# Branch outputs loaded into the buffer of their lower parts and split there; queries of a head loaded once

## The chip, the core and the metric

The program runs on one core of a Trainium2 chip. The core has a matrix engine (PE, with a separate queue for loading weights, PEld), a vector engine (DVE), a scalar engine (ACT), GpSimd (POOL), and SyncE (SP), from which nearly all transfers of this program are issued to 16 shared DMA engines. The metric is the device time of one execution in microseconds, the median over several runs.

## What is computed

One layer of an encoder over two sequences, of 1024 and 2048 tokens, each with 16 learned tokens in front. Only the skeleton is shown; all arithmetic is float32.

```python
xn = _rmsnorm(h, g_pre)
proj = xn @ w_in + b_in                      # 1024 -> 6672 columns
na_q, na_k, na_v, na_z, ml_qk, ml_v, ml_z, ml_o, ml_g, mg = jnp.split(proj, SPLIT_IDX, axis=-1)
ya = _neighbourhood_attention(q, k, v, na_rpb)   # 8 heads of 64, windows of 8 x 16 on a grid 64 wide
ya = (ya * silu(na_z)) @ w_a
yb = (_mlstm_branch(ml_qk, ml_v, ml_g, ml_o, conv_w, head_g) * silu(ml_z)) @ w_b   # 4 heads of 128
ga, gb = split(sigmoid(mg))
y = (ga * ya + gb * yb) @ w_out
return h + _rmsnorm(y, g_post)
```

## The kernel before

To keep float32 accuracy each operand of a matmul is split in two: an upper part, which ACT makes by copying to a shorter format (`yh`, `xh`, `whi`, `mh`), and a lower part, the rest, which DVE makes by subtracting (`yl`, `xl`, `wlo`, `mlo`). A product is three matmuls, upper by upper, upper by lower, lower by upper (L155 to L157, L577 to L579, L1497 to L1499).

Two generators run beside each other. `dense` makes the projections and the end of the layer; `sparse` makes the mLSTM branch (`ml`) and the attention (`na`). `run` takes steps of both in turn, by costs written in the code, and this fixes the order of the PE's instructions. The order on the other engines and on SP's queue is made by a planner when the program is built: it plays the program through with its own times, and an instruction whose data and buffers are ready by these times may be put far ahead of its place in the code. Each queue then runs in that order, and an instruction that has to wait holds up all that stand behind it on its engine.

The end of the layer is `final(s, b, nxt)`, six blocks of 512 tokens: two of the first sequence, four of the second. A block has two stages. In the first, called the branch stage here, the outputs of both branches (`y`, eight slices k of 128 features; k = 4 to 7 are the mLSTM's, k = 0 to 3 the attention's) are multiplied by `w_a` and `w_b`, gated (DVE, L1467 and L1469) and split into `mh` and `mlo` (ACT L1470, DVE L1471). In the second, the output projection, `mh` and `mlo` are multiplied by `w_out` in 16 units of 128 tokens by 256 columns, each followed by ACT L1524 and DVE L1525. While the blocks are made the attention of the second sequence still runs, 32 heads one after another; one query block of a head takes the PE through scores (L849), ACT through the exponential (L857), DVE through scaling (L866), the PE through a transpose (L874), ACT and DVE through the split of the result (L876, L877), and the PE and both again through the output (L886, L890, L892).

`yload(s, b)` brings the outputs of the branches from DRAM for a block. It is started in the output projection of the block before (for the first block in the last projection job before it), and stepped once for each unit (`hook`). Before, a slice is loaded to a buffer `yr` (L1418) with the tag `st`, which has four buffers that the gates `tg` and other stages use as well; when three slices are under way the oldest is split: ACT copies `yr` to `yh[:, k]` (L1405), DVE subtracts into `yl[:, k]` (L1406). The buffers `yh` and `yl` share their tags with `xh` and `xl`, two each: the next block's `yl` takes the place of this block's `yl`, which is free when the branch stage has ended.

`na_prep` prepares a head of the attention one head ahead. `twice` loads a matrix of 64 rows to both halves of the partitions, which is used for the queries (`qr`, L733 twice) and the keys (`kr`). ACT then copies `qr` to `stk` on 128 partitions (L824), copies the upper 64 partitions' result to `qB` (L826), and DVE subtracts on partitions 64 to 127, so that `stk` holds upper parts above and lower parts below (L827). Keys go the same way (L829, L831), values in L834 and L836.

Of the kernel before, what the change touches and what calls it, by code (L numbers as in the profile page):

```python
# [9 lines left out]
F32 = mybir.dt.float32  # L10
F32R = mybir.dt.float32r
I32 = mybir.dt.int32
AF = mybir.ActivationFunctionType
ALU = mybir.AluOpType
# [3 lines left out]
P = 128  # L18
# [102 lines left out]
class K:  # L121
# [671 lines left out]
    def na_prep(self, np_, s, rows, heads, j):  # L793

        nc, i = self.nc, self.i
        rt, pr, hh = heads[j]
        typ, lo, nr = rows[rt]
        ns, h0 = nr + 1, hh * 64
        ms, rs = ((nr, 0), (nr, 0), (0, 1))[typ]
        qr = np_.tile([P, 512], F32, name="qr", bufs=1)  # L800
        stk = np_.tile([P, 4, P], F32R, name="stk", bufs=2)
        qb = self.qB[hh]
        self.twice(qr, self.NQ[s][pr], h0, rt * 512)
        sv = stk.rearrange("p b t -> p (b t)")
        kr = np_.tile([P, 16, 64], F32, name="kr", bufs=1)
        kd = np_.tile([P, 16, 64], F32R, name="kd", bufs=2)
        kx = self.kx[hh]
        self.twice(kr[:, rs:rs + nr, :].rearrange("p a b -> p (a b)"), self.NK[s][pr], h0, lo * 64)
        self.twice(kr[:, ms, :], self.NKM[pr], h0, 0)
        ks = 8 * ns  # L810
        if hh == 0:
            self.vr = np_.tile([P, 8, P], F32, name="vr", bufs=1)
            f0 = pr * P
            nc.sync.dma_start(self.vr[ms * 8:ms * 8 + 8], self.NVM[:, f0:f0 + P].rearrange("(b c) f -> c b f", c=8))
            nc.sync.dma_start(self.vr[rs * 8:(rs + nr) * 8],
                              self.NV[s][:, lo * 8:(lo + nr) * 8, f0:f0 + P].rearrange("b q f -> q b f"))
            self.zt = np_.tile([P, 512], F32, name="zt", bufs=2)
            nc.sync.dma_start(self.zt, self.NZ[s][pr][:, rt * 512:(rt + 1) * 512])
            self.yg = np_.tile([P, 512], F32, name="yg", bufs=2)
        vr, zt, yg = self.vr, self.zt, self.yg  # L820
        if j < 2 or rows[heads[j - 2][0]][0] != typ:
            nc.gpsimd.dma_start(kx[64:128, :ns, :].rearrange("p a b -> p (a b)"), i["masks"][typ, :, :ns * 64])
        yield
        nc.scalar.activation(sv, qr, AF.Copy)  # L824
        yield
        nc.scalar.activation(qb[0:64], stk[0:64].bitcast(F32), AF.Copy)  # L826
        nc.vector.tensor_tensor(sv[64:128], qr[64:128], sv[64:128].bitcast(F32), op=ALU.subtract)  # L827
        yield
        nc.scalar.activation(kd[:, :ns, :], kr[:, :ns, :], AF.Copy)  # L829
        yield  # L830
        nc.vector.tensor_tensor(kx[0:64, :ns, :], kr[0:64, :ns, :], kd[0:64, :ns, :].bitcast(F32), op=ALU.subtract)  # L831
        vt = np_.tile([P, 8, 2, 64], F32R, name="vt", bufs=2)
        vv = vr[:ks, :, h0:h0 + 64]
        nc.scalar.activation(vt[:ks, :, 0], vv, AF.Copy)  # L834
        yield
        nc.vector.tensor_tensor(vt[:ks, :, 1], vv, vt[:ks, :, 0].bitcast(F32), op=ALU.subtract)  # L836
        self.head = stk, qb, kd, vt, yg, zt
        yield
# [556 lines left out]
    def yload(self, s, b):  # L1395

        nc, fp, n = self.nc, self.wp, 512
        yh = fp.tile([P, KT, n], F32R, name="yh", tag="xh", bufs=2)
        yl = fp.tile([P, KT, n], F32R, name="yl", tag="xl", bufs=2)
        self.y, self.yk = ((s, b), yh, yl), set()  # L1400
        todo = deque()

        def split():
            k, yr = todo.popleft()
            nc.scalar.activation(yh[:, k], yr, AF.Copy)  # L1405
            nc.vector.tensor_tensor(yl[:, k], yr, yh[:, k].bitcast(F32), op=ALU.subtract)  # L1406
            self.yk.add(k)

        for k in (4, 5, 6, 7, 0, 1, 2, 3):
            need = ("ml", s) if k > 3 else ("na", s, b, k)  # L1410
            if need not in self.done:
                while todo:
                    split()
                    yield
                while need not in self.done:
                    yield "wait"
            yr = fp.tile([P, n], F32, name="yr", tag="st", bufs=4)
            nc.sync.dma_start(yr, self.YA[s][b][k][:, :] if k < 4 else self.YB[s][k - 4][:, b * n:(b + 1) * n])  # L1418
            todo.append((k, yr))
            if len(todo) == 3:  # L1420
                split()
                yield
        while todo:
            split()
            yield

    def ystart(self, s, b):
        self.ygen = self.yload(s, b)
# [269 lines left out]
```

## Time and profile before

| | |
|---|---|
| median of 3 runs | 2843.53 us (2842.91 to 2847.38) |
| the profiled execution, its own time | 2845.39 us |
| its span, first to last instruction | 2843.6 us |
| granted clock of the PE, mean | 0.994 |
| DMA | 661.42 MB, mean 233 GB/s |

The profile's page gives the busy time of each engine. The view of stretches gives the same for any window, with the clock that the PE was granted (1.00 is full) and the mean busy share of the DMA engines. The view of waits sums the idle time of an engine by the line that waited and the work that ended the wait: total us, number of times, longest. In the view in order of time a row has its start, its duration, engine and line, and in square brackets the idle time of that engine just before it and what ended this.

### The profile page before, as it was taken

What the parts mean: (1) busy time and instruction counts of PE and PEld (TensorE: products, weight loads), DVE (VectorE), ACT (ScalarE), POOL (GpSimd) and SP (SyncE); (2) the same over time, 40 slices, a digit from 0 to 9 for tenths busy, and PEclk for the clock granted to TensorE, in tenths of its full rate; (3) what the DMA queues carried; (4) which work ended last, traced back from release to release, by engine and by line L of the source; (5) the groups of instructions that cost most, each with busy time, mean ns of one, the idle gap of its engine ahead of it and who ended that gap; (6) DMA issues with size and microseconds to landing.
All of it is one profiled execution on the core that took longest, in us unless ns stands there. A gap on an engine that the chain in (4) does not pass through costs nothing.

```text
span 2843.6 us, 49257 instructions
## 1 busy us (share of the span) xinstructions
PE 2795.7 (98%) x17312; PEld 2488.8 (88%) x17312; DVE 1796.3 (63%) x4931; ACT 1306.4 (46%) x3135; POOL 16.1 (1%) x103
## 2 busy tenths in 40 slices
PE   9999999999999999999999999999999999999998
PEld 8998898999899988888988888888888988889898
DVE  5233678576456654456667566474679888787854
ACT  5122546444444443355455555453455554545421
POOL 0000000000000000000000000000000000000000
PEclk9999999999999999999999999999999999999999
DMA  9554768765966554685656776656679999897875
GB/s 373 186 186 178 261 210 300 252 196 165 343 210 192 169 173 131 189 281 181 210 176 224 251 274 193 185 171 180 196 239 355 308 308 279 286 291 258 290 259 193
DMA packets 382120, 661.42 MB, mean 233 GB/s; under 512 B 51664, under 2 KB 200608, under 8 KB 381872
## 3 DMA queue, kind: packets, MB, share of 16 engines
q1 hardware_dynamic: 380752, 655.58, 69.7%
q0 software_dynamic: 1120, 2.69, 0.4%
q8 instruction: 137, 2.24, 0.3%
q14 instruction: 111, 0.91, 0.1%
HBM read 455.90 MB, written 202.22 MB: 231 GB/s over the span
## 4 chain that ended last, share of the span: by engine, by line
PE 85%; DMA 8%; DVE 5%; ACT 1%; issue 1%; SPq 0%; DVEq 0%; ACTq 0%
PE pj L155 15%; PE pj L156 14%; PE pj L157 14%; PE pj L577 6%; PE pj L578 6%; PE pj L579 6%; PE pj L1499 3%; PE pj L1497 3%; PE pj L1498 3%; PE sm L886 3%; PE tr L874 2%; DMA wlo<-wl 1%; DMA um<-ud 1%; PE sm L157 1%; PE sc L849 1%; PE sm L156 1%
## 5 line engine op out<-in xcount | busy, mean ns | idle before, releaser
L155 PE MATMUL pj<-xh,whi 128*128 128x512 f32 (+1 forms) x1792 | 705.7, 394 | 0.9 <-ACT whi L250 0.9
L156 PE MATMUL pj<-xl,whi 128*128 128x512 f32 (+1 forms) x1792 | 689.5, 385 | 0.1
L157 PE MATMUL pj<-xh,wlo 128*128 128x512 f32 (+1 forms) x1792 | 688.2, 384 | 0.3 <-DVE wlo L251 0.3
L577 PE MATMUL pj<-whi,xh 128*128 128x256 f32 (+3 forms) x1576 | 451.2, 286 | 4.4 <-DMA whi<-wh 2.9
L578 PE MATMUL pj<-wlo,xh 128*128 128x256 f32 (+3 forms) x1576 | 445.1, 282 | 0.8 <-DMA wlo<-wl 0.8
L579 PE MATMUL pj<-whi,xl 128*128 128x256 f32 (+3 forms) x1576 | 444.6, 282 | 0.0
L157 PEld LDWEIGHTS pj<-xh,wlo 128*128 128x128 f32 x1792 | 337.2, 188 | 72.1 <-DVE wlo L251 0.5
L155 PEld LDWEIGHTS pj<-xh,whi 128*128 128x128 f32 x1792 | 337.7, 188 | 60.5 <-ACT whi L250 1.7
L156 PEld LDWEIGHTS pj<-xl,whi 128*128 128x128 f32 x1792 | 338.0, 189 | 56.9 <-issue 1.0
L577 PEld LDWEIGHTS pj<-whi,xh 128*128 128x128 f32 (+1 forms) x1576 | 294.5, 187 | 6.4 <-DMA whi<-wh 3.1
L578 PEld LDWEIGHTS pj<-wlo,xh 128*128 128x128 f32 (+1 forms) x1576 | 294.3, 187 | 2.1 <-DMA wlo<-wl 1.1
L579 PEld LDWEIGHTS pj<-whi,xl 128*128 128x128 f32 (+1 forms) x1576 | 294.3, 187 | 0.9
L1497 PE MATMUL pj<-whi,mh 128*128 128x256 f32 x768 | 220.9, 288 | 4.2 <-DMA whi<-wh 2.4
L1499 PE MATMUL pj<-whi,mlo 128*128 128x256 f32 x768 | 217.5, 283 | 1.1 <-DVE mlo L1471 1.1
L1498 PE MATMUL pj<-wlo,mh 128*128 128x256 f32 x768 | 217.5, 283 | 0.1
L857 ACT ACTIVATE prb<-sc,mx 128x384 f32<-128x384 f32 (+2 forms) x192 | 119.8, 624 | 204.2 <-DVE mx L853 193.2
L877 DVE TENSOR_TENSOR pts<-tr,pts 96x512 fp32r<-96x512 f32 (+2 forms) x192 | 131.5, 685 | 75.8 <-ACT pts L876 74.3
L876 ACT ACTIVATE pts<-tr 96x512 fp32r<-96x512 f32 (+2 forms) x192 | 113.9, 593 | 114.8 <-PE tr L874 113.5
L155 PE MATMUL pj<-yh,whi 128*128 128x512 f32 x384 | 155.9, 406 | 0.0
L156 PE MATMUL pj<-yl,whi 128*128 128x512 f32 x384 | 152.2, 396 | 0.0
L157 PE MATMUL pj<-yh,wlo 128*128 128x512 f32 x384 | 152.2, 396 | 0.0
L1497 PEld LDWEIGHTS pj<-whi,mh 128*128 128x128 f32 x768 | 146.3, 190 | 6.5 <-ACT mh L1470 2.3
(271 smaller groups left out, 5049.4 us busy)
## 6 DMA issues: line engine op xcount, KB each, us to landing
whi<-wh SPq DMA_DIRECT2D x176, 512.0 KB
wlo<-wl SPq DMA_DIRECT2D x176, 512.0 KB
wraw<-wu SPq DMA_DIRECT2D x64, 512.0 KB
wh<-whi SPq DMA_DIRECT2D x64, 512.0 KB
wl<-wlo SPq DMA_DIRECT2D x64, 512.0 KB
gt<-st SPq DMA_DIRECT2D x96, 256.0 KB
tg<-gt SPq DMA_DIRECT2D x96, 256.0 KB
xt<-xt SPq DMA_DIRECT2D x32, 512.0 KB
```

The lines of the kernel that those rows point to most:

```text
L155: mm(out, ah, bh, start=start, stop=False)
L156: mm(out, ah, bl, start=False, stop=False)
L157: mm(out, al, bh, start=False, stop=stop)
L577: nc.tensor.matmul(o, xh, wh, start=k == 0, stop=False)
L578: nc.tensor.matmul(o, xh, wl, start=False, stop=False)
L579: nc.tensor.matmul(o, xl, wh, start=False, stop=k == KT - 1)
L857: nc.scalar.activation(pr_[:, :N].rearrange("p (b a c) -> p b a c", b=4, c=8), sc[:, :N].rearrange("p (a b c) -> p b a c", b=4, c=8), AF.E ...
L876: nc.scalar.activation(pts[:ks, :, 0, :], pt[:ks], AF.Copy)
L877: nc.vector.tensor_tensor(pts[:ks, :, 1, :], pt[:ks], pts[:ks, :, 0, :].bitcast(F32), op=ALU.subtract)
L1497: nc.tensor.matmul(o, mh[:, k, xs], wh, start=k == 0, stop=False)
L1498: nc.tensor.matmul(o, mh[:, k, xs], wl, start=False, stop=False)
L1499: nc.tensor.matmul(o, ml[:, k, xs], wh, start=False, stop=k == KT - 1)
```

## The change

In `yload` the buffer `yr` is gone. A slice is loaded straight into `yl[:, k]`; ACT copies it from there to `yh[:, k]`, and DVE subtracts in place. All slices that are ready in DRAM when the generator starts are loaded at its first step; six empty steps follow, and then one split at a step. Slices that are not ready are kept in `late` and loaded when they are, with two empty steps behind each. In `na_prep` the queries are loaded once, to partitions 0 to 63; ACT copies those 64 partitions, and DVE reads partitions 0 to 63 and writes 64 to 127. Loads of the keys stay as they are.

```diff
@@ -800,7 +800,7 @@
         qr = np_.tile([P, 512], F32, name="qr", bufs=1)
         stk = np_.tile([P, 4, P], F32R, name="stk", bufs=2)
         qb = self.qB[hh]
-        self.twice(qr, self.NQ[s][pr], h0, rt * 512)
+        nc.sync.dma_start(qr[0:64], self.NQ[s][pr][h0:h0 + 64, rt * 512:(rt + 1) * 512])
         sv = stk.rearrange("p b t -> p (b t)")
...
         yield
-        nc.scalar.activation(sv, qr, AF.Copy)
+        nc.scalar.activation(sv[0:64], qr[0:64], AF.Copy)
         yield
         nc.scalar.activation(qb[0:64], stk[0:64].bitcast(F32), AF.Copy)
-        nc.vector.tensor_tensor(sv[64:128], qr[64:128], sv[64:128].bitcast(F32), op=ALU.subtract)
+        nc.vector.tensor_tensor(sv[64:128], qr[0:64], sv[0:64].bitcast(F32), op=ALU.subtract)
...
@@ -1400,29 +1400,34 @@
         self.y, self.yk = ((s, b), yh, yl), set()
         todo = deque()
 
+        def load(k):
+            nc.sync.dma_start(yl[:, k].bitcast(F32), self.YA[s][b][k][:, :] if k < 4 else self.YB[s][k - 4][:, b * n:(b + 1) * n])
+            todo.append(k)
+
         def split():
-            k, yr = todo.popleft()
-            nc.scalar.activation(yh[:, k], yr, AF.Copy)
-            nc.vector.tensor_tensor(yl[:, k], yr, yh[:, k].bitcast(F32), op=ALU.subtract)
+            k = todo.popleft()
+            nc.scalar.activation(yh[:, k], yl[:, k].bitcast(F32), AF.Copy)
+            nc.vector.tensor_tensor(yl[:, k], yl[:, k].bitcast(F32), yh[:, k].bitcast(F32), op=ALU.subtract)
             self.yk.add(k)
 
+        late = []
         for k in (4, 5, 6, 7, 0, 1, 2, 3):
-            need = ("ml", s) if k > 3 else ("na", s, b, k)
-            if need not in self.done:
-                while todo:
-                    split()
-                    yield
-                while need not in self.done:
-                    yield "wait"
-            yr = fp.tile([P, n], F32, name="yr", tag="st", bufs=4)
-            nc.sync.dma_start(yr, self.YA[s][b][k][:, :] if k < 4 else self.YB[s][k - 4][:, b * n:(b + 1) * n])
-            todo.append((k, yr))
-            if len(todo) == 3:
+            if (("ml", s) if k > 3 else ("na", s, b, k)) in self.done:
+                load(k)
+            else:
+                late.append(k)
+        for _ in range(6):
+            yield
+        while todo or late:
+            while late and (("ml", s) if late[0] > 3 else ("na", s, b, late[0])) in self.done:
+                load(late.pop(0))
+                for _ in range(2):
+                    yield
+            if todo:
                 split()
                 yield
-        while todo:
-            split()
-            yield
+            else:
+                yield "wait"
```

## The prediction

> **What bounds the kernel.** I began with the page's first part.
>
> ```profile
> span 2843.6 us, 49257 instructions
> ...
> PE 2795.7 (98%) x17312; PEld 2488.8 (88%) x17312; DVE 1796.3 (63%) x4931; ACT 1306.4 (46%) x3135; POOL 16.1 (1%) x103
> ```
>
> The matrix engine is busy in all but 2843.6 - 2795.7 = 47.9 us, and the change takes no matmul away and moves none: the steps of `yload` carry no cost in `run`, so the order on the PE stays. The change can act only through the PE's idle time, and through the clock that goes down after some of it. So next I asked where the PE waits while the six blocks of the end are made, first by stretches (columns: stretch, its length, busy time of PE, PEld, DVE, ACT, POOL, granted clock, DMA share, GB/s). The first row is a branch stage, the second an output projection beside attention, the third one at the end of the attention.
>
> ```profile
> 2128.00:2191.00 63.00, 60.09 (x295) 49.46 (x294) 57.43 (x116) 35.04 (x66) 0.51 (x1) 0.97 1.03 352
> ...
> 2312.00:2375.00 63.00, 61.20 (x495) 59.86 (x494) 45.31 (x110) 35.76 (x95) 0.00 (x0) 1.00 0.84 251
> ...
> 2689.00:2742.00 53.00, 53.00 (x444) 52.87 (x443) 25.95 (x65) 20.33 (x62) 0.00 (x0) 1.00 0.58 198
> ```
>
> In a branch stage DVE works 57.43 of 63 us and the DMA engines are full; in an output projection both have room. The waits of the PE from 2090 to 2740 us, and those of ACT for the buffer that the change removes:
>
> ```profile
> PE tr L874 <- DVE prb L866: 12.3, 7, 3.3
> PE sc L849 <- ACT prb L857: 5.5, 3, 3.0
> ```
>
> ```profile
> ACT yh L1405 <- DMA yr<-yb: 21.9, 11, 3.9
> ...
> ACT yh L1405 <- DMA yr<-ya: 13.4, 10, 2.6
> ```
>
> ACT stands 35.3 us in front of a slice that has not landed, 21 times for 48 slices. That matters only where the PE then waits. In order of time, the PE's waits that end in ACT's work, or in what ACT's work feeds:
>
> ```profile
> 2324.06 0.50 PE L849 MATMUL sc<-kd,stk 128*128 128x512 f32 x1 [1.80 <-ACT prb L857]
> ...
> 2444.27 0.39 PE L1497 MATMUL pj<-whi,mh 128*128 128x256 f32 x1 [1.81 <-ACT mh L1470]
> ...
> 2445.59 0.39 PE L1499 MATMUL pj<-whi,mlo 128*128 128x256 f32 x1 [0.82 <-DVE mlo L1471]
> ...
> 2572.86 0.71 PE L849 MATMUL sc<-kd,stk 128*128 128x416 f32 x1 [2.96 <-ACT prb L857]
> ```
>
> and what ACT did just before each:
>
> ```profile
> 2313.00 0.62 ACT L1405 ACTIVATE yh<-yr 128x512 fp32r<-128x512 f32 x1
> 2313.95 0.63 ACT L1405 ACTIVATE yh<-yr 128x512 fp32r<-128x512 f32 x1 [0.34 <-DMA yr<-yb]
> ...
> 2316.64 0.62 ACT L834 ACTIVATE vt<-vr 128x512 fp32r<-128x512 f32 x1
> 2321.17 0.63 ACT L1405 ACTIVATE yh<-yr 128x512 fp32r<-128x512 f32 x1 [3.91 <-DMA yr<-yb]
> ...
> 2322.32 0.38 ACT L1524 ACTIVATE yo<-pj 128x256 f32<-128x256 f32 x1
> ...
> 2442.58 0.63 ACT L1405 ACTIVATE yh<-yr 128x512 fp32r<-128x512 f32 x1 [3.80 <-DMA yr<-yb]
> ...
> 2569.63 0.63 ACT L1405 ACTIVATE yh<-yr 128x512 fp32r<-128x512 f32 x1 [2.31 <-DMA yr<-yb]
> ```
>
> Each time ACT's queue is held by a slice under way; the exponential or `mh` behind it is late, and the PE stops. The other large sum, L874 behind DVE's L866 (12.3 us), lies mostly in the branch stages, where DVE is nearly full. The change takes no DVE instruction away, so I leave that sum where it is.
>
> **The stalls removed.** 1.80 + (1.81 + 0.82) + 2.96 = 7.4 us directly. The clock adds to it:
>
> ```profile
> 780.00:800.00 20.00, 16.34 (x92) 14.94 (x91) 7.21 (x18) 5.03 (x11) 0.00 (x0) 0.83 0.99 308
> ```
>
> ```profile
> 2322.00:2342.00 20.00, 18.20 (x149) 17.70 (x148) 17.06 (x42) 13.86 (x39) 0.00 (x0) 1.00 0.90 272
> 2440.00:2460.00 20.00, 17.37 (x126) 16.53 (x126) 14.01 (x34) 11.03 (x28) 0.00 (x0) 0.91 1.02 290
> 2565.00:2585.00 20.00, 17.04 (x129) 16.79 (x128) 16.08 (x36) 12.56 (x32) 0.00 (x0) 0.91 0.92 304
> ```
>
> After the stall of 1.80 us the clock stays at 1.00. After the 2.63 and the 2.96 us it falls to 0.91 over 20 us, which is 0.09 x 20 = 1.8 us of PE work lost each time. Gross gain: 7.4 + 3.6 = 11.0 us.
>
> The Trainium skill, "TensorE: Matmul & The Clock Gate", section "Part 1: The HAM clock gate (the "warmup" mystery)", lets the clock fall to half after an idle window of some 3.4 us. By that figure none of these three stalls would cost clock, and the gain would stop at 7.4 us; the rows at 2440 and 2565 show the drop after shorter stalls, and the measurement decides.
>
> **What comes in their place.** The first slices are loaded early now because `yr` is a separate buffer. Afterwards no slice can be asked for before the last matmul of the branch stage has read the old `yl`, so all eight go out together at the start of the output projection, behind each other on SP. The six empty steps set a later place in the code, but the queue is planned by readiness: the three splits between 2313 and 2322 us stand ahead of the block's first unit (L1524 at 2322.32), where the code has all of them behind it. So I expect ACT to come to the first slice before it has landed, once per output projection. Its price follows from how long a slice takes: issue on SP to ACT's release for three that ACT stood waiting for.
>
> ```profile
> 2315.22 0.33 SPq L1418 DMA_DIRECT2D yr<-yb  x1
> ...
> 2436.69 0.32 SPq L1418 DMA_DIRECT2D yr<-yb  x1
> ...
> 2561.08 0.54 SPq L1418 DMA_DIRECT2D yr<-yb  x1
> ```
>
> 2321.17 - 2315.22 = 5.95, 2442.58 - 2436.69 = 5.89, 2569.63 - 2561.08 = 8.55; mean 6.8 us. The first split at 2313.00 marks the buffers coming free. ACT then had work until 2316.64 + 0.62 = 2317.26, which is 4.26 us, 1.25 of it splits that the change puts later; 3.0 us of own work remain. With 0.3 us for the issue ACT would stand 6.8 + 0.3 - 3.0 = 4.1 us. Of 3.91 us the PE felt 1.80, so 2.1 us are slack, and 4.1 us cost 2.0 us of PE, near the 1.80 that left the clock alone. Five output projections lie beside attention; three pay today, and I take three again: 6.0 us. The bounds: none pays (0), or four pay at the longest landing, 8.55 + 0.3 - 3.0 - 2.1 = 3.75 us of stall and 1.8 us of clock, 5.5 x 4 = 22 us.
>
> The other parts cost nothing on the path:
>
> ```profile
> L1405 ACT ACTIVATE yh<-yr x48: 612/632/636, 2100.8 to 2730.2; 128x512 fp32r<-128x512 f32 x48
> L1406 DVE TENSOR_TENSOR yl<-yr,yh x48: 673/684/694, 2101.5 to 2730.9; 128x512 fp32r<-128x512 f32 x48
> ```
>
> ```profile
> L1469 DVE TENSOR_TENSOR tg<-tg 128x512 f32<-128x512 f32 x40 | 27.3, 683 | 0.2
> ```
>
> ```profile
> L733 SPq DMA_DIRECT2D qr<-nq x96: 445/451/1425, 752.3 to 2646.4; - x96
> L824 ACT ACTIVATE stk<-qr x48: 615/632/635, 760.5 to 2664.6; 128x512 fp32r<-128x512 f32 x48
> L827 DVE TENSOR_TENSOR stk<-qr,stk x48: 678/689/691, 761.2 to 2666.2; 64x512 fp32r<-64x512 f32 x48
> ```
>
> A split keeps its two instructions; in place costs DVE the same (L1469, in place, 683 ns against 684). The queries lose 48 of 96 loads of 128 KB: 6.3 MB, about 1% of the 661 MB, and 48 x 0.45 = 22 us of SP, which runs beside the PE. The cover is that the loads are issued a head ahead. ACT's copy has the same 512 elements on half the partitions, DVE's subtraction the same shape with another half as source; no row has exactly that, and the nearest, L827 itself, says 689 ns. I take no change for both; their ends are 0 and a gain where the DMA engines hold up the PE directly, at the start of the first attention:
>
> ```profile
> PE pj L577 <- DMA whi<-wh: 2.9, 1, 2.9
> PE pj L578 <- DMA wlo<-wl: 0.8, 1, 0.8
> ```
>
> With the clock of that stretch, 0.83 over 20 us, that is 3.7 + 3.4 = 7.1 us at most; two doubled query loads stand ahead of those weights in the queue, too little to clear 2.9 us, so I take 0.
>
> Sum: -11.0 + 6.0 = -5.0 us. The profiled execution took 2845.39 us in all and would come to 2840.4; it lies 1.9 us above the median 2843.53, so the median would come to 2838.5 us.
>
> **Rivals.** *All waits for slices go.* If the planner leaves the splits at their late places, ACT never stands: -11.0 us, and with half of the 7.1 us for the weights -14.5: 2829 us. For it: six empty steps are six units, far more than 8.55 us. Against it: the three splits planned ahead of their places.
>
> *The burst behind the release costs more than it saves* (slower). One mechanism: eight slices, 2 MB, are queued at the moment the old `yl` is released, at the end of a stage in which the DMA engines are at 1.03, and ACT stands in front of the first. It decides from about 7.2 us of landing: then ACT stands 4.5 us, the stall is 2.4 us, between the 1.80 that left the clock and the 2.63 that did not, and four of 2.4 + 1.8 = 4.2 us outweigh 11.0. At the longest landing it gives +22 - 11 = +11: 2854.5 us. For it: one of three landings was 8.55. Against it: an output projection has DMA room (0.84, 0.58).
>
> "DMA: Bandwidth & Descriptors" of the Trainium skill, section "Rules for kernel authors", advises issuing a load early and waiting for it late. The change waits later by its code and issues later by its buffer; the second half speaks for this rival.
>
> *The gain is taken up elsewhere.* The planner orders DVE and ACT anew, and the 12.3 us behind L866, which hang on this order in stages with DVE at 57.43 of 63, grow by what the slices gave. 2843 us, no change. For it: that sum is the largest. Against it: nothing there grows longer.
>
> *It does not do what it says:* if the slices of one buffer waited for each other, the first split would wait for the eighth load, 2 MB at the 251 GB/s of that stage or 8.4 us more: 45 us for four, +34 us, 2877 us. Against it: the PE worked on slices of `mh` while the last was still awaited at 2444.27.
>
> **How the numbers follow.** The forecast has 0.44, about 2833 to 2843 us; all waits gone 0.12; the burst 0.30; taken up elsewhere 0.12; not what it says 0.02. A measurement of this kernel tells 0.2%, or 5.7 us, from no change. The forecast lies near that bound: 0.28 faster, 0.16 same. Faster: 0.28 + 0.12 = 0.40. Same: 0.16 + 0.10 = 0.26. Slower: 0.30 + 0.02 + 0.02 = 0.34. The range takes in most of the waits-gone case and the burst at its full price, 2827 to 2856 us; the forecast's own is 2833 to 2843.
>
> **What would show it.** Right: eight loads into `yl` side by side on SP at each start of an output projection; ACT's waits for them below 35.3 us; the PE's waits on L857, `mh` and `mlo` down from 7.4 to about 6 us, none followed by a drop of the clock. The splits at 0.63 and 0.68 us as now; query loads x48. Wrong: waits of ACT over 4.5 us with the clock at 0.91 behind them (the burst); no wait of ACT for slices (the first rival); L874 behind L866 well off 12.3 us (the planner's order).

## The result, and the profile after

| | before | after |
|---|---|---|
| median of 4 runs | 2845.45 us (2842.91 to 2847.86) | 2862.34 us (2860.62 to 2866.52) |
| the profiled execution, its own time | 2845.39 us | 2866.52 us |
| mean granted clock | 0.994 | 0.991 |

The ratio is 1.0053, with an interval of 1.0029 to 1.0078: the kernel became slower by about half a per cent, 15 us. 2838.5 us had been forecast, in a range of 2827 to 2856.

The first part of the page of the kernel after:

```profile
span 2864.7 us, 49167 instructions
...
PE 2799.0 (98%) x17312; PEld 2490.2 (87%) x17312; DVE 1799.0 (63%) x4931; ACT 1306.8 (46%) x3135; POOL 15.8 (1%) x103
```

The matmuls are the same 17312. The PE's idle time went from 47.9 us to 2864.7 - 2799.0 = 65.7 us, 17.8 us more, and its work from 2795.7 to 2799.0 us, 3.3 us more for the same matmuls at a lower clock. Together these are the 21.1 us by which the spans of the two profiled executions differ. The other engines do what they did before. So the loss is stalls of the PE, and the clock behind them.

The waits of the PE and of ACT while the six blocks are made (2090 to 2763 us in the kernel after; columns as before: sum, times, longest):

```profile
PE tr L874 <- DVE prb L866: 24.2, 12, 4.4
PE sc L849 <- ACT prb L857: 11.4, 4, 7.9
...
PE pj L1502 <- DVE yo L1530: 1.7, 1, 1.7
```

```profile
ACT yh L1409 <- DMA yl<-yb: 20.4, 8, 9.0
...
ACT yh L1409 <- DMA yl<-ya: 1.8, 2, 1.4
```

ACT's waits for slices fell from 35.3 to 22.2 us, as forecast, and yet the PE's two large sums doubled, from 12.3 + 5.5 to 24.2 + 11.4 us. The sum of ACT's waits was not what the PE feels. Their longest went from 3.9 to 9.0 us, and a wait costs the PE only what exceeds its slack.

The slices of a block are loaded and split in the output projection of the block before it, for the first block at the end of the last projection job. These stretches are called load stages here; the output projections begin at 2203, 2331, 2456, 2587 and 2711 us. Where the PE stood, in order of time (start, duration, and in brackets the idle time just before and the instruction that ended it): the stalls over 0.6 us of the load stages, and one of a branch stage at 2290:

```profile
2111.61 0.45 PE L849 MATMUL sc<-kd,stk 128*128 128x384 f32 x1 [1.77 <-ACT prb L857]
...
2117.83 1.06 PE L874 MATMUL tr<-ident,prb 128*96 128x128 f32 x4 [3.58 <-DVE prb L866]
...
2221.02 0.63 PE L874 MATMUL tr<-ident,prb 128*128 128x128 f32 x4 [1.40 <-DVE prb L866]
...
2228.32 0.63 PE L874 MATMUL tr<-ident,prb 128*128 128x128 f32 x4 [1.45 <-DVE prb L866]
...
2290.63 1.09 PE L874 MATMUL tr<-ident,prb 128*128 128x128 f32 x4 [4.43 <-DVE prb L866]
...
2341.75 0.50 PE L849 MATMUL sc<-kd,stk 128*128 128x512 f32 x1 [1.13 <-ACT prb L857]
...
2348.31 0.51 PE L849 MATMUL sc<-kd,stk 128*128 128x512 f32 x1 [0.62 <-ACT prb L857]
...
2352.76 0.63 PE L874 MATMUL tr<-ident,prb 128*128 128x128 f32 x4 [0.87 <-DVE prb L866]
...
2475.04 0.79 PE L849 MATMUL sc<-kd,stk 128*128 128x512 f32 x1 [7.86 <-ACT prb L857]
...
2600.39 0.39 PE L1502 MATMUL pj<-whi,mh 128*128 128x256 f32 x1 [1.75 <-DVE yo L1530]
```

The load stages have 1.77 + 3.58 + 1.40 + 1.45 + 1.13 + 0.62 + 0.87 + 7.86 + 1.75 = 20.4 us of idle time, for 5.5 + 2.6 = 8.1 us in the kernel before. Four of these stalls are on L866, 7.3 us; outside of the load stages L866 has 24.2 - 7.3 = 16.9 us, for 12.3. So of the 17.8 us more 12.3 us come from the load stages and 4.6 us from L866 in the branch stages.

The load stages by stretches, with the granted clock third from the right:

```profile
2100.00:2120.00 20.00, 14.64 (x68) 11.49 (x67) 15.41 (x33) 13.23 (x26) 0.51 (x1) 0.82 0.89 280
2460.00:2480.00 20.00, 12.14 (x88) 11.65 (x88) 11.05 (x24) 10.42 (x26) 0.00 (x0) 0.83 1.00 315
```

A low clock costs the PE only where it works. In windows of 1 us the clock of the first stretch is at 0.50 from about 2112.8 to 2123.0 us; in 3.58 us of that the PE stands, and in the other 6.6 us it works at half speed, which is 3.3 us lost. With the stalls of 1.77 + 3.58 us that is 8.7 us. In the second stretch the clock is at 0.50 from 2471.2 to 2478.0 us, but the PE works again only from 2475.04: 3.0 us at half speed (its matmuls L1502 to L1504 start 0.21 us apart there, and 0.12 us apart from 2478 on), 1.5 us lost, 9.4 us with the stall of 7.86. The kernel before lost little at the first place:

```profile
2100.00:2120.00 20.00, 19.30 (x100) 15.84 (x99) 17.42 (x37) 14.26 (x28) 0.51 (x1) 1.00 0.95 284
```

**The largest stall.** SP's queue at the end of the branch stage before 2460 us, and ACT's queue there, with its longest waits in two other projections:

```profile
2456.87 0.32 SPq L243 DMA_DIRECT2D whi<-wh  x1
...
2457.77 1.02 SPq L1452 DMA_DIRECT2D tg<-gt  x2
...
2459.36 0.39 SPq L243 DMA_DIRECT2D wlo<-wl  x1
2459.80 2.74 SPq L1404 DMA_DIRECT2D yl<-yb  x4
```

```profile
2339.41 0.63 ACT L1409 ACTIVATE yh<-yl 128x512 fp32r<-128x512 f32 x1 [3.79 <-DMA yl<-yb]
...
2459.89 0.58 ACT L876 ACTIVATE pts<-tr 128x512 fp32r<-128x512 f32 x1
2469.51 0.63 ACT L1409 ACTIVATE yh<-yl 128x512 fp32r<-128x512 f32 x1 [9.04 <-DMA yl<-yb]
...
2595.89 0.63 ACT L1409 ACTIVATE yh<-yl 128x512 fp32r<-128x512 f32 x1 [3.74 <-DMA yl<-yb]
```

The first slice is asked for at 2459.80, behind weights and gates, with the DMA engines at 1.00 of their time. It lands by 2469.51, 9.7 us later. ACT was done at 2459.89 + 0.58 = 2460.47 and stood in front of it for 9.04 us; the exponential that the PE waited for was queued behind. The waits of 3.79 and 3.74 us stand ahead of the stalls of 1.13 and 1.75 us in two other output projections, where the first slice, issued at 2333.52 and 2588.10, took 5.9 and 7.8 us.

**The first load stage.** ACT's splits for the first block:

```profile
2101.36 0.64 ACT L1409 ACTIVATE yh<-yl 128x512 fp32r<-128x512 f32 x1 [0.32 <-DMA yl<-yb]
...
2105.25 0.63 ACT L1409 ACTIVATE yh<-yl 128x512 fp32r<-128x512 f32 x1 [2.25 <-DMA yl<-yb]
...
2106.74 1.14 ACT L1409 ACTIVATE yh<-yl 128x512 fp32r<-128x512 f32 x2
2108.28 0.63 ACT L1409 ACTIVATE yh<-yl 128x512 fp32r<-128x512 f32 x1 [0.40 <-DMA yl<-ya]
...
2111.45 0.62 ACT L1409 ACTIVATE yh<-yl 128x512 fp32r<-128x512 f32 x1
```

Eight splits stand within 10.7 us. ACT waited only some 3 us for loads in all; the rest is the work of a run that stands ahead of what the attention needs. The scaling L866 for which the PE stands 3.58 us starts at 2117.28; DVE has worked without a gap since 2105.91, and of these 11.4 us six subtractions L1410 take 4.0 us. The splits of weights, keys, queries and values stand in the same row.

**A stall that is not the slices'.** At 2286 us DVE waits, for the input rows `xres` that the end of the block before adds to its output:

```profile
2286.01 1.41 DVE L1576 SCALAR_TENSOR_TENSOR yo<-yo,nwy,xres 128x512 f32<-128x512 f32 x2 [3.50 <-DMA xres<-x_prompt]
```

L1576 is L1571 of the kernel before. The scaling L866 that the PE's transpose needs at 2290.63 is queued behind it.

### The profile page after: what moved, and what is told of

Its sections match the earlier page's. It is cut to its first block, busy times and chain, and to the rows that moved or that the text cites. A ratio compares the mean times of both kernels' runs of the same rounds, so it can differ in the third digit from the quotient of the medians.

```text
span 2864.7 us, 49167 instructions
## 1 busy us (share of the span) xinstructions
PE 2799.0 (98%) x17312; PEld 2490.2 (87%) x17312; DVE 1799.0 (63%) x4931; ACT 1306.8 (46%) x3135; POOL 15.8 (1%) x103
## 3 DMA queue, kind: packets, MB, share of 16 engines
q0 software_dynamic: 1120, 2.69, 0.4%
## 4 chain that ended last, share of the span: by engine, by line
PE 81%; DMA 9%; DVE 6%; ACT 1%; issue 1%; SPq 1%; DVEq 0%; ACTq 0%
PE pj L155 14%; PE pj L156 14%; PE pj L157 14%; PE pj L577 6%; PE pj L578 6%; PE pj L579 6%; PE pj L1502 3%; PE pj L1503 3%; PE pj L1504 3%; PE sm L886 3%; PE tr L874 2%; DMA um<-ud 2%; DMA wlo<-wl 2%; PE sm L157 1%; PE sm L156 1%
## 5 line engine op out<-in xcount | busy, mean ns | idle before, releaser
L1502 PE MATMUL pj<-whi,mh 128*128 128x256 f32 x768 | 220.9, 288 | 3.7 <-DMA whi<-wh 2.0
L1504 PE MATMUL pj<-whi,mlo 128*128 128x256 f32 x768 | 217.3, 283 | 0.0
L857 ACT ACTIVATE prb<-sc,mx 128x384 f32<-128x384 f32 (+2 forms) x192 | 119.8, 624 | 205.7 <-DVE mx L853 194.5
L877 DVE TENSOR_TENSOR pts<-tr,pts 96x512 fp32r<-96x512 f32 (+2 forms) x192 | 131.6, 685 | 82.2 <-ACT pts L876 80.5
L1502 PEld LDWEIGHTS pj<-whi,mh 128*128 128x128 f32 x768 | 146.4, 191 | 6.0 <-DVE yo L1530 2.0
```

The lines of the kernel that those rows point to most:

```text
L857: nc.scalar.activation(pr_[:, :N].rearrange("p (b a c) -> p b a c", b=4, c=8), sc[:, :N].rearrange("p (a b c) -> p b a c", b=4, c=8), AF.E ...
L877: nc.vector.tensor_tensor(pts[:ks, :, 1, :], pt[:ks], pts[:ks, :, 0, :].bitcast(F32), op=ALU.subtract)
L1502: nc.tensor.matmul(o, mh[:, k, xs], wh, start=k == 0, stop=False)
L1504: nc.tensor.matmul(o, ml[:, k, xs], wh, start=False, stop=k == KT - 1)
```

## The experiments

All twelve were timed against the kernel before on the same chip; E1 to E4 ran together, E5 to E8, E9 to E11, and E12 by itself.

| | kernel | us | before, same chip | ratio (interval) |
|---|---|---|---|---|
| E1 | before, queries loaded once | 2853.92 | 2847.22 | 1.0028 (1.0014 to 1.0043) |
| E2 | before, new `yload` | 2855.26 | 2847.22 | 1.0030 (1.0016 to 1.0044) |
| E3 | after, copies of slices held | 2839.74 | 2847.22 | 0.9971 (0.9959 to 0.9983) |
| E4 | after, splits on GpSimd | 2849.41 | 2847.22 | 1.0007 (0.9993 to 1.0020) |
| E5 | before, new form of the queries, both loads | 2846.56 | 2842.34 | 1.0010 (0.9996 to 1.0023) |
| E6 | before, copies of slices held | 2833.30 | 2842.34 | 0.9967 (0.9950 to 0.9985) |
| E7 | new `yload` held, queries loaded twice | 2832.50 | 2842.34 | 0.9968 (0.9951 to 0.9985) |
| E8 | in place, but with the old steps | 2851.47 | 2842.34 | 1.0039 (1.0023 to 1.0055) |
| E9 | before held, queries loaded once | 2840.56 | 2846.32 | 0.9970 (0.9957 to 0.9983) |
| E10 | before, copies and residuals held | 2825.25 | 2846.32 | 0.9928 (0.9906 to 0.9950) |
| E11 | after, copies and residuals held | 2828.46 | 2846.32 | 0.9932 (0.9915 to 0.9948) |
| E12 | after, first copy held, seven right behind | 2846.99 | 2845.13 | 1.0002 (0.9987 to 1.0017) |

### E1 and E2: each half of the change alone

E1 has the part in `na_prep` alone, E2 the part in `yload` alone.

```diff
-        self.twice(qr, self.NQ[s][pr], h0, rt * 512)
+        nc.sync.dma_start(qr[0:64], self.NQ[s][pr][h0:h0 + 64, rt * 512:(rt + 1) * 512])
...
-        nc.scalar.activation(sv, qr, AF.Copy)
+        nc.scalar.activation(sv[0:64], qr[0:64], AF.Copy)
...
-        nc.vector.tensor_tensor(sv[64:128], qr[64:128], sv[64:128].bitcast(F32), op=ALU.subtract)
+        nc.vector.tensor_tensor(sv[64:128], qr[0:64], sv[0:64].bitcast(F32), op=ALU.subtract)
```

> The kernel before with the query loads of the change alone; yload as before. Theory A (the slices cost the time: loads that can only start when the old lower parts are released, and eight splits planned right behind them): about as before, 2845 us, at most +3, because only the stall on weights near 788 us (3.7 us before, 5.3 us after) can belong to the queries; ACT's waits for yr stay near 35 us. Rival B (the queries shift the planned order and cost the time): +10 us or more, 2856 us and up.

For E2 the three lines above are as in the kernel before, and all else is as after. The first lines of this:

```diff
-            k, yr = todo.popleft()
-            nc.scalar.activation(yh[:, k], yr, AF.Copy)
+            k = todo.popleft()
+            nc.scalar.activation(yh[:, k], yl[:, k].bitcast(F32), AF.Copy)
```

> The kernel before with the new yload alone; queries loaded twice as before. Theory A: within 4 us of the changed kernel, 2858 to 2866 us, with a wait of ACT of more than 5 us for a first slice in at least one output projection and a stall of the PE behind it. Rival B: near the kernel before, 2843 to 2849 us.

Each half costs: 0.28% and 0.30%, and 0.28 + 0.30 = 0.58 is near the 0.53% of both. Both theories missed E1: its 0.28%, some 8 us, lies between the next to nothing of the one and the 10 us or more of the other. E2 came between its two as well, nearer to the first; the sign that theory A gave, a wait of ACT of more than 5 us, was just missed at 4.7. The PE stands 3.89 us at 2461 us, behind one of ACT's waits of 4.25 us, as A had it, but most of its added idle time is on L866, 22.3 us for 12.3. ACT's waits for slices in E2:

```profile
ACT yh L1409 <- DMA yl<-yb: 14.8, 8, 4.7
```

In E1 nothing of `yload` is touched, and still the PE's sum on L866 is 19.4 us, from 12.3. SP, DVE and PE around its largest stall:

```profile
2269.66 0.34 SPq L1556 DMA_DIRECT2D xres<-x_prompt  x1
```

```profile
2271.15 0.69 DVE L877 TENSOR_TENSOR pts<-tr,pts 128x512 fp32r<-128x512 f32 x1
2275.22 1.42 DVE L1571 SCALAR_TENSOR_TENSOR yo<-yo,nwy,xres 128x512 f32<-128x512 f32 x2 [3.38 <-DMA xres<-x_prompt]
```

```profile
2279.84 1.09 PE L874 MATMUL tr<-ident,prb 128*128 128x128 f32 x4 [4.31 <-DVE prb L866]
```

And the same load in the kernel before:

```profile
2265.36 0.34 SPq L1556 DMA_DIRECT2D xres<-x_prompt  x1
```

```profile
2267.59 0.69 DVE L877 TENSOR_TENSOR pts<-tr,pts 128x512 fp32r<-128x512 f32 x1
...
2270.49 0.47 DVE L866 TENSOR_SCALAR prb<-prb,sm 128x512 f32<-128x512 f32 x1
...
2271.09 1.40 DVE L1571 SCALAR_TENSOR_TENSOR yo<-yo,nwy,xres 128x512 f32<-128x512 f32 x2
```

From issue to DVE's start it is 2275.22 - 2269.66 = 5.6 us in E1. Before it is 2271.09 - 2265.36 = 5.7 us, and there DVE did not wait, so the rows had landed by then. Before, DVE did other work in that time, L866 among it; in E1 the planner put the addition straight behind L877, and L866 behind the addition. The same stall is in every kernel with the queries loaded once whose additions are left to the planner: 4.31 us in E1, 5.00 in E3, 4.49 in E4, 4.19 in E9, 4.43 in the kernel after, and 2.96 in E12. With the queries loaded twice the stalls of the PE in this stretch are 1.4 to 2.6 us (before, E2, E5 to E8). So one load less for each head was enough for another order of DVE. Why the planner chose it is not shown.

### E3: the copies of the slices held in the queue's order

The planner can be given an edge: an instruction may not be put ahead of a named one in its queue. The edge is on the order of issue alone; nobody waits for the named one's end. Here ACT's copy of a slice may not stand ahead of the last exponential (L857) or squaring (L1529) that precedes it in the code. It undoes the planner's early placing and leaves the loads, the buffers and the work alone.

```diff
-        nc.scalar.activation(pr_[:, :N].rearrange("p (b a c) -> p b a c", b=4, c=8),
+        self.at = nc.scalar.activation(pr_[:, :N].rearrange("p (b a c) -> p b a c", b=4, c=8),
...
-            nc.scalar.activation(yh[:, k], yl[:, k].bitcast(F32), AF.Copy)
+            with self.tc.issue_after(self.at.ins):
+                nc.scalar.activation(yh[:, k], yl[:, k].bitcast(F32), AF.Copy)
...
-                nc.scalar.activation(dst, o, AF.Square, accum_out=ssq[:, tt, cq:cq + 1])
+                self.at = nc.scalar.activation(dst, o, AF.Square, accum_out=ssq[:, tt, cq:cq + 1])
```

> The changed kernel, but ACT's copy of a slice is kept in issue order behind the last exponential (L857) or squaring of a unit (L1529) that the code has in front of it, so the planner cannot put it ahead. Loads as in the change. Theory A: ACT's waits for slices fall from 22.2 us to under 3 us, the PE's stalls at the first load stage (5.4 us and 5.1 us of clock), at 2467 us (7.9 us and 3.4 us of clock) and around 2220 and 2345 us (5.5 us) go: 27 us less at the most, 2838 to 2848 us. Rival C (any new order of ACT and DVE costs this much, the waits for slices are only one face of it): still 2855 us or more.

2839.74 us, 0.29% below the kernel before and some 0.8% below the kernel after. The PE's waits from 2080 to 2760 us:

```profile
PE tr L874 <- DVE prb L866: 18.0, 9, 5.0
PE pj L1503 <- DMA whi<-wh: 1.3, 2, 0.9
```

As theory A had it, the 11.4 us on L857 are gone, and ACT waits for no slice. The loads still wait for the same release of `yl`; what was added between 1.0053 and 0.9971 is the edge on the copies alone. The planner ordered the rest anew around it. What stays hangs on L866, 5.0 us of it in the stall behind `xres`.

### E4: the splits on GpSimd

```diff
-            nc.scalar.activation(yh[:, k], yl[:, k].bitcast(F32), AF.Copy)
-            nc.vector.tensor_tensor(yl[:, k], yl[:, k].bitcast(F32), yh[:, k].bitcast(F32), op=ALU.subtract)
+            nc.gpsimd.tensor_copy(yh[:, k], yl[:, k].bitcast(F32))
+            nc.gpsimd.tensor_tensor(yl[:, k], yl[:, k].bitcast(F32), yh[:, k].bitcast(F32), op=ALU.subtract)
```

> The changed kernel with copy and subtraction of a slice both on GpSimd, which is idle for 99% of the span; the planner may put them where it likes, and a late slice holds up GpSimd alone. Theory A: no wait of ACT or DVE for slices, and 48 x 0.63 us of ACT and 48 x 0.68 us of DVE taken off: 2833 to 2845 us, less if DVE is not slowed by GpSimd. Rival C: 2855 us or more. If it is the traffic of the eight loads that delays the attention's own loads or the weights, the time stays near 2855 us too, but with the PE or DVE waiting for DMA.

1.0007, with 1 in the interval: between the two theories. Its groups on GpSimd (busy us, mean ns), and two of the PE's waits from 2080 to 2770 us:

```profile
L1410 POOL TENSOR_TENSOR yl<-yl,yh 128x512 fp32r<-128x512 f32 x48 | 68.4, 1444 | 0.2
L1409 POOL CAST yh<-yl 128x512 fp32r<-128x512 f32 x48 | 34.5, 737 | 643.9 <-DMA yl<-yb 568.8 <-PE sm L886 54.1 <-DMA yl<-ya 20.9
```

```profile
PE tr L874 <- DVE prb L866: 19.5, 10, 4.5
PE sc L849 <- ACT prb L857: 3.4, 1, 3.4
```

GpSimd spends 103 us on the splits and stands 569 + 21 us in front of slices with nobody behind it, and there is no stall of 7.86 us any more. But taking 48 subtractions from DVE left 19.5 us behind L866: that sum is not made by the splits alone.

### E5: the form of the queries with both loads kept

The second and third edit of E1, without the first.

```diff
-        nc.scalar.activation(sv, qr, AF.Copy)
+        nc.scalar.activation(sv[0:64], qr[0:64], AF.Copy)
```

> The kernel before with the copy and the subtraction of the queries in the changed form (64 partitions copied, DVE from the lower half to the upper), but with both loads of the queries kept; the second load's data is read by nobody. Theory D (the changed form costs nothing; what cost 8 us with the queries is that one load fewer shifts all later loads and splits in the planned order): as before, within 3 us of it. Rival E (DVE's read from the other half or ACT's copy of 64 partitions is slow or holds up its neighbours): +5 to +8 us, with L827 longer than 0.69 us or gaps behind it.

1.0010, with 1 in the interval. The DVE row of it:

```profile
L827 DVE TENSOR_TENSOR stk<-qr,stk x48: 684/685/687, 760.8 to 2665.4; 64x512 fp32r<-64x512 f32 x48
```

Read from the other half of the partitions, the subtraction takes 685 ns, against 689 before. As expected by D, the form costs nothing that can be told, so what E1 lost came, as far as the runs tell it, with the load that was left out. The intervals of E1 (from 1.0014) and E5 (to 1.0023) overlap a little.

### E6, E7 and E9: holding without the change, and with each half of it

E6 is the kernel before with the edge of E3 around its own copy. E7 is E3 with the queries loaded twice. E9 is E6 with the three edits of E1.

```diff
-            nc.scalar.activation(yh[:, k], yr, AF.Copy)
+            with self.tc.issue_after(self.at.ins):
+                nc.scalar.activation(yh[:, k], yr, AF.Copy)
```

> The kernel before, changed in one thing: ACT's copy of a slice is kept behind the last exponential or squaring that the code has in front of it. Theory A (what costs is ACT being planned ahead of slices under way): the stalls at 2322, 2443 and 2570 us with their clock, 11 us, go; 7 to 12 us below the kernel before. Rival F (the gain of the held kernel came from the in-place loads, which leave the buffers of the gates alone, and not from holding): within 3 us of the kernel before.

> The new yload with ACT's copies held, queries loaded twice as before. If the queries cost 8 us whatever stands beside them: 8 us below the held kernel with single queries, that is 2829 to 2834 us beside 2847 for the kernel before. If they cost only by way of the order that they happen to give: between 2834 and 2845 us, in no fixed relation to it.

> The kernel before with ACT's copies of slices held at their place and the queries loaded once. Theory D (one load fewer costs nothing by itself; its 8 us came from slices and other planned-ahead work falling badly in the new order): within 4 us of the held kernel with both loads, so 0.2 to 0.45% below the kernel before. Rival (single query loads cost by themselves, whatever the order): 8 us above it, 0 to 0.1% below the kernel before.

0.9967, 0.9968 and 0.9970, beside 0.9971 for E3: with the copies held, all four combinations take the same time within their intervals. E6 and E7 ran on one chip, 2833.30 and 2832.50 us: slices loaded in place cost nothing, and gain nothing. E7's 2832.50 us falls by its number in the lower range of its expectation, but that range was meant beside 2847 us for the kernel before, and this chip has 2842.34; 0.9968 of 2847 is 2838 us, in the other range (the queries cost only by way of the order). In E6 the PE's only wait of weight, and ACT's, from 2085 to 2735 us:

```profile
PE tr L874 <- DVE prb L866: 11.8, 8, 3.6
```

```profile
ACT yh L1406 <- DMA yr<-ya: 8.7, 6, 2.1
```

ACT still stands 8.7 us in front of these slices and 1.6 us in front of the others, and the PE feels none of it: the 5.5 us on L857 and the 2.6 us on `mh` and `mlo` are gone. For the queries the answer is less sharp. E9 equals E6 by the ratios, as theory D had it, but E9's profile still has the stall behind `xres`, 4.19 us of the PE at 2271.86. That the single load by itself neither costs nor saves more than some 0.2% is what the two intervals allow.

### E8: in place, but with the old steps

Slices go straight into `yl[:, k]`, and the loop is the old one: a split when three are under way, no empty steps.

```diff
-            yr = fp.tile([P, n], F32, name="yr", tag="st", bufs=4)
-            nc.sync.dma_start(yr, self.YA[s][b][k][:, :] if k < 4 else self.YB[s][k - 4][:, b * n:(b + 1) * n])
-            todo.append((k, yr))
+            nc.sync.dma_start(yl[:, k].bitcast(F32), self.YA[s][b][k][:, :] if k < 4 else self.YB[s][k - 4][:, b * n:(b + 1) * n])
+            todo.append(k)
```

> Slices loaded straight into yl and split in place, but with the old steps: a load, and a split as soon as three are under way, no empty steps. Queries twice. Theory A (the planner goes by readiness, so the six empty steps and the loads put first have no effect, and the release of yl sets the time of the loads): within 4 us of the new yload alone, so 0.2 to 0.5% above the kernel before, with waits of ACT for slices of 15 us or more. Rival G (the loads put first, eight in a burst, are what costs): back at the kernel before, within 3 us.

1.0039, against 1.0030 of E2 on another chip: the six empty steps do nothing measurable, as A expected. ACT's waits for slices are 14.4 us, for 15 or more expected, and the longest is 3.2 us; the PE's sum on L866 is 21.5 us. What E2 and E8 have in common is the buffer, which ties the loads to the release of the old `yl`. It costs only while the copies may be planned ahead: in E7 they are held, and it costs nothing.

### E10 and E11: the residual additions held too

DVE's additions L1571 (L1576 in the kernel after) get an edge of the same kind: none ahead of the last scaling (L866) or split of a transpose (L877) that precedes it in the code. E10 is E6 with it, E11 is E3 with it.

```diff
-        nc.vector.tensor_scalar(pr_[:, :N], pr_[:, :N], sm, None, op0=ALU.mult)
+        self.dt = nc.vector.tensor_scalar(pr_[:, :N], pr_[:, :N], sm, None, op0=ALU.mult)
...
-        nc.vector.tensor_tensor(pts[:ks, :, 1, :], pt[:ks], pts[:ks, :, 0, :].bitcast(F32), op=ALU.subtract)
+        self.dt = nc.vector.tensor_tensor(pts[:ks, :, 1, :], pt[:ks], pts[:ks, :, 0, :].bitcast(F32), op=ALU.subtract)
...
-                nc.vector.scalar_tensor_tensor(y, y, r[:, tt - a:tt - a + 1], self.last.pop(0) if self.last else x[:, c], op0=ALU.mult, op1=ALU.add)
+                with self.tc.issue_after(self.dt.ins):
+                    nc.vector.scalar_tensor_tensor(y, y, r[:, tt - a:tt - a + 1], self.last.pop(0) if self.last else x[:, c], op0=ALU.mult, op1=ALU.add)
```

> The kernel before with ACT's copies held, and on DVE the additions of the residual (L1571) held behind the last scaling (L866) or subtraction (L877) of the attention that the code has in front of them. Theory H (the same thing on DVE: an addition planned ahead of a residual under way, or simply ahead of the attention, is what is left of the stalls on L866): the waits of the PE on L866 fall from 11.8 us to under 6 us, 4 to 8 us below the kernel with ACT's copies held alone, 2826 to 2832 us beside 2845. Rival I (these stalls come from DVE being full in the branch stages, whatever the order): within 3 us of it.

> The changed kernel with both held. Theory H: its wait of 5.0 us near 2272 us, behind an addition that waits for its residual, goes; 4 to 8 us below the changed kernel with ACT's copies held alone, and within 4 us of the kernel before with both held. Rival I: within 3 us of the changed kernel with ACT's copies held, 0.3% below the kernel before.

0.9928 and 0.9932: both beat the kernel before and the kernel after, E10 by 0.72% and 1.2%. The direction and the sum on L866 are as H expected; the gain over the kernels with the copies alone held, 0.39% or some 11 us across chips, is more than its 4 to 8 us. The PE's waits in E10 from 2090 to 2716 us, and the page's first part:

```profile
PE tr L874 <- DVE prb L866: 4.2, 4, 1.9
PE sc L849 <- ACT prb L857: 2.0, 4, 1.0
```

```profile
span 2817.4 us, 49270 instructions
...
PE 2784.5 (99%) x17312; PEld 2480.2 (88%) x17312; DVE 1794.4 (64%) x4931; ACT 1308.2 (46%) x3135; POOL 15.7 (1%) x103
```

The sum on L866 fell from 11.8 us in E6 to 4.2 us with no work taken from DVE (4931 instructions in both). The idle time of the PE is 2817.4 - 2784.5 = 32.9 us, and its work 2784.5 us, 11.2 us less than before for the same matmuls, at a mean clock of 0.998 for 0.994: with fewer stalls there are fewer drops of the clock. The profiled execution took 2819.18 us, 6 us under the median of E10. In E11 one addition still waits 5.25 us for `xres`, at 2415 us, and the PE stands 3.33 us behind it: an edge to a place in the code does not wait for the landing.

### E12: a run of eight without the waits

E3 with another edge: only the first copy of a block is held, and the other seven may come right behind it. This keeps the run of splits and takes the waits in front of slices away (all but one of 1.7 us).

```diff
-            with self.tc.issue_after(self.at.ins):
-                nc.scalar.activation(yh[:, k], yl[:, k].bitcast(F32), AF.Copy)
+            with self.tc.issue_after((first or [self.at])[0].ins):
+                first.append(nc.scalar.activation(yh[:, k], yl[:, k].bitcast(F32), AF.Copy))
...
-        late = []
+        late, first = [], []
```

> The changed kernel, with the first copy of a block kept at its place in the code and the other seven only behind it, so that all eight come one after another on ACT, long after their loads have landed: no wait for a slice, but a run of eight. Theory A1 (the waits for loads under way do the harm): as with all copies held at their places, 0.2 to 0.4% below the kernel before. Theory A2 (the run of splits does it, by keeping ACT and DVE from the attention): each of five or six blocks stalls the PE by 2 to 4 us, 10 to 20 us above the held kernel, 0.1 to 0.4% above the kernel before, with no wait of ACT for a slice in the trace.

1.0002, between the two theories: 0.3% above E3, in which the copies lie apart, and 0.5% below the kernel after. ACT and PE around one run, and the stretch:

```profile
2343.45 3.23 ACT L1410 ACTIVATE yh<-yl 128x512 fp32r<-128x512 f32 x6
...
2347.54 1.13 ACT L1410 ACTIVATE yh<-yl 128x512 fp32r<-128x512 f32 x2
```

```profile
2355.21 1.09 PE L874 MATMUL tr<-ident,prb 128*128 128x128 f32 x4 [2.69 <-DVE prb L866]
```

```profile
2340.00:2360.00 20.00, 17.31 (x131) 16.94 (x131) 16.12 (x36) 13.18 (x34) 0.00 (x0) 0.91 0.87 253
```

No slice is waited for in this run, and the PE still loses 2.69 us and 0.09 x 20 = 1.8 us of clock: L866 starts at 2354.58, after DVE has worked without a gap since 2344.11, 5.1 us of it on the eight subtractions. So the run seems to have a price of its own, about 0.3%, and the waits in front of slices one of about 0.5%. Each is a difference between kernels whose queues the planner ordered anew, taken on different chips, so by the intervals the first share holds to some 0.2% and the second to some 0.3%.

## Why the prediction was wrong

**What bounds the kernel: right.** The PE's matmuls and their number are unchanged, and the whole difference is its idle time and its clock. ACT's queue held by a slice under way was the right mechanism too: E6, whose one edge keeps the copies from standing early, is at 0.9967, 9.4 us of its 2842.34 (4.3 to 14.2 by the interval). The 11.0 us of the stalls removed fit that.

**What comes in their place: this step failed.** It put one wait in each output projection at 4.1 us, gave three of them a cost of 2.0 us and left the clock alone, 6.0 us in all. The load stages lost 20.4 us of stalls, and clock besides. Three projections paid for a wait, as counted: 1.13, 7.86 and 1.75 us, 10.7 in all. Two are near the term, with waits of 3.79 and 3.74 us; one is four times the term:
- The landing was taken as 6.8 us, from three slices that ACT had waited for before, single loads among others. The first slices of the bursts took 5.9, 9.7 and 7.8 us, the longest behind weights and gates. Why that one took longest is not shown.
- ACT's own work between issue and first split was taken as 3.0 us from one projection. At 2460 us it was 2460.47 - 2459.80 = 0.67 us (2.1 and 4.1 us in the other two). So ACT stood 9.04 us, not 4.1.
- Of these the PE felt 7.86 us, so the slack was 1.2 us, where 2.1 had been read off a single stall, and the clock fell.

The step also had no line for two things. The load stage of the first block, ahead of the first branch stage, was not counted at all, and lost 8.7 us with its clock. And eight splits in a run were costed as eight splits, when they also hold up what is queued behind them on ACT and on DVE (E12, about 0.3%): 1.40 + 1.45 + 0.62 + 0.87 = 4.3 us of the stalls above have splits in the row ahead of them and no wait of ACT for a slice. Nor do the traces bear out the bound that the step took for the clock, between stalls of 1.80 and 2.63 us: in the kernel after it falls behind the stall of 1.75 us at 2600 and stays at 1.00 behind one of 3.07 us at 2671.

**The queries at nothing: wrong, though each price was right.** The subtraction takes 685 ns for 689 (E5), and with the copies held the saved loads neither gain nor cost (E9). What was put at nothing is the planner's new order around a load that is gone. E1 costs 0.28%, and its trace shows DVE in front of `xres` and the PE's sum on L857 at 8.9 us for 5.5. How much of the 0.28% is which stays open: E9 keeps the stall behind `xres` and loses nothing against E6 that can be told. The rival "taken up elsewhere" named that order, but only as big enough to take up the gain. In the kernel after, the stall of 4.43 us at 2290.63 is this one.

**The 12.3 us on L866 left where they are: wrong.** They were read as the load of DVE in a branch stage, 57.43 of 63 us. E10 brings the sum to 4.2 us with the same instructions on DVE. Most of it went when the additions alone were held, so it was order, not load.

**The rivals.** The burst behind the release had the direction, the place and the signs (a wait of ACT over 4.5 us: 9.04; the clock down behind it: 0.83), and its decisive point, 7.2 us of landing, was passed in two of three projections. Its price was built from four stalls of 3.75 us; there was one of 7.86 and two under 2 us, and the rest came from the first load stage, from the runs and from the branch stages. So it had the place and the direction right and the sum only in part. That all waits go, which the forecast gave 0.12, did happen as soon as the copies were held (E3), with 0.9971 for the hoped-for 0.995. The slices of one buffer did not wait for each other: ACT took the first at 2101.36, when the last four were still being issued.

The Trainium skill's rule cited in the prediction ("DMA: Bandwidth & Descriptors", "Rules for kernel authors": issue early, wait late) is borne out in its second half. The change waits late in the code, but its planned order waited early; E3 and E12 put the wait later and gained 0.8% and 0.5%. The first half cannot be told here: with the copies held, slices issued early (E6) and late (E7) take the same time.

**What would have shown it.** One question was not asked of the trace before: by what time the planner thinks a load lands. In the rows of the prediction a slice is issued at 2315.22, ACT is ready for it at 2316.64 + 0.62 = 2317.26, and it lands at 2321.17. So the planner seems to have counted on about 2 us where the chip took 6; its own times are not on record. If so, any load that is issued later brings its wait closer to the front.

## What to carry to other kernels

Where an order of queues is planned from estimates, look at the longest wait in front of a load and at what is queued behind it, not at the sum of such waits: 22.2 us of waits cost more here than 35.3. A buffer that is loaded in place moves the load to the release of its old contents, and costs if the first reader is not kept behind other work for the whole of the real landing time, here up to 9.7 us. With the reader kept there it gained nothing here either (E7 beside E6). And any edit, even one that removes work, may reorder queues elsewhere; before believing or rejecting it, hold the order of the instructions that wait for transfers (here one edge each for ACT and DVE, -0.72%), and compare again.

## What was not expected of the hardware

- In the kernel after, the first slice of a block, 256 KB, was there 2.6 us after its issue in the first load stage, with the DMA engines at 0.6 of their time, and 5.9, 7.8 and 9.7 us after it in three output projections, with the engines at 0.98 to 1.03. Leaving out 48 loads of 128 KB saved no time that can be told (E9 against E6).
- The clock fell after short stalls, and the length of one stall does not tell whether it will: 0.91 over 20 us after 2.69 us (E12) and after 1.75 us (2590 to 2610 us in the kernel after), but 1.00 after 1.80 us in the kernel before, after 2.96 us in E12 (2270 to 2290 us) and after 3.07 us in the kernel after (2660 to 2680 us). What does decide is not shown. The Trainium skill, "TensorE: Matmul & The Clock Gate", "Part 1: The HAM clock gate (the "warmup" mystery)", puts the idle window at about 3.4 us; the 7.86 us of the kernel after agree with it, the drops after 2.69 and 1.75 us do not.
- GpSimd takes 737 ns for a copy and 1444 ns for a subtraction of 128x512 (E4), against 0.63 us on ACT and 0.68 us on DVE in the kernel before. It is slow, but it can stand in front of a transfer where nobody is queued behind.
